# Hybrid streaming encoder on one core: operand buffers at first write, one scratch buffer per builder, and sums given to the engine that ends first

## The chip, the cores and the metric

The kernel runs on one core of a Trainium2 chip. The metric is device time in microseconds of one execution. Three runs of the kernel before gave 2709.64 to 2714.51 us, median 2712.25.

## The reference, cut to what matters

Two layers run over 1024 prompt tokens and 32 sample tokens (1056 columns in all), model width 1024. Each layer has a normalised input projection, latent attention beside retention, an output projection, then the feed-forward part and a gated embedding. The feed-forward part comes once per layer, behind the output projection:

```python
mix = jnp.concatenate([att, retention_out(ret, rg, ret_gn_w[i])], axis=-1)
hp = hp + mix @ w_out[i]                                  # output projection
u = rms_norm(h, norm_ffn_w) @ w_ff1                       # 1024 -> 4096
h = h + jnp.square(jax.nn.relu(u)) @ w_ff2                # 4096 -> 1024
gate = jax.nn.sigmoid(rms_norm(h, norm_ple_w) @ w_ple_gate)
return h + (p_i @ w_ple_proj) * gate
```

## The kernel before, in words

**A planner writes the program.** The Python code of the kernel carries a model of the five engines (`Model`, line 72; `Engine.cost`, line 263). Chains of work are generators; `Pipe` steps each when its next operation could start by the model, and the order in which operations are emitted is the order in which each engine executes them. So a wait in the planner (`pipe.wait`, or a `yield` of a condition) is no wait on the chip: it decides behind what an instruction is written. Matmuls are emitted in line and move the planner's clock; DMAs go to SP's queue. Two-operand sums that VectorE (DVE) or GpSimd (POOL) can do are `Either` (line 202), made by `tt(first, ...)` (line 461): the engine listed first is taken if it can start no more than 0.2 us later than the other.

**Numbers.** Every matmul operand is kept as a high and a low half in f16, and a product is three matmuls per 128 rows: high by high, high by low, low by high. A "split" is the pair of instructions that makes the halves: ScalarE (ACT) casts the high half, and a subtraction by DVE or POOL gives the low half.

**The feed-forward products.** Both matrices are multiplied in blocks of two by two with seven products in place of eight. For this the right operands are seven combinations of the four quarters of the activation (y11, y21, y12, y22 and the sums s1 = y21 + y22, s2 = s1 - y11, s3 = y11 - y21, s4 = y12 - s2), called operands 0 to 6 in the order y11, y12, y22, s1, s2, s3, s4, and the weights have seven combinations too. `load_group` (line 801) fetches four weight blocks, makes four sums with `tt(pool, ...)`, and writes seven weight tiles by `put`. Products are done in the order 1, 7, 6, 4, 5, 2, 3, reading operands 0, 5, 4, 2, 3, 1, 6. 

**The order of a layer's feed-forward part.** Lines 1783 to 1809: the output projection runs over three token groups (2 x 176 columns each), and behind each group `norm_chain` (line 631) squares the rows (ACT), adds them over partitions (TensorE with ones), takes the power -0.5 (POOL), scales a diagonal (ACT) and spreads it by a product with ones, and then four `four` chains (line 717) write operands "x2": two scaled rows, four sums, and four splits, of which (0,5), (1,2) and (4,6) go as pairs. Then come four blocks e; each has four first groups (`ff1_units`, line 943, writing output operands "r") and four second ones (`ff2_units`, line 965, adding into h). The first two groups of block 0 run together, token group by token group, so two units alternate; all other groups run over two halves of 264 columns. `ff1_chains` (line 870) evacuates the products of a unit, squares them and makes sums and splits: ACT copies the first product to `lo` of scratch Ra, and `c11` (line 915) makes s3 and s2 after s1, splitting them as the pair (4,5).

**Buffers.** The arena has 29 slots of 128 x 2 x 1056 f16, weights have 14 slots, temps (128 x 528 f32) 12. x2 takes 14 arena slots, the output operands of two groups 7, a group's staged weights 1, and during the output projection weights may spill into arena halves ("we"). Line 1880 waits for seven free slots before the output operands of two groups are taken, line 746 for temps and a slot before a `four` starts, and only then line 1884 lets the third group's weights load.

## Time and profile before

| what | value |
|---|---|
| runs, median (lowest to highest) | 2712.25 us (2709.64 to 2714.51) |
| the profiled execution, own time | 2710.96 us |
| its span, first to last instruction | 2709.2 us |
| mean granted TensorE clock | 0.974 |
| instructions | 58534 |

In the views, PE is the matmul side of TensorE, DVE VectorE, ACT ScalarE, POOL GpSimd, SP the DMA queue. Times are microseconds from the span's start. Almost every vector instruction is recorded at line 285 and every matmul at line 476, so rows are told apart by tile names (out<-in), with numbers left out of the names: "x" holds x2, "r" is both a scratch buffer of the norm and an output operand, "ra" and "rb" are scratch of a unit, "st", "o", "mm" and "mx" are PSUM banks.

### The profile page before, as it was taken

How to read it: one execution, taken by the hardware profiler on the slowest of the kernel's cores; microseconds unless marked ns; L12 is line 12 of the kernel's file. 1: busy time of each engine (PE TensorE's matmuls, PEld its weight loads, DVE VectorE, ACT ScalarE, POOL GpSimd, SP SyncE). 2: the span in 40 equal slices, each digit the busy share in tenths (PEclk: the TensorE clock that was granted, in tenths of full speed). 3: DMA queues.
4: the chain of work that ended last, by engine and by line, in shares of the span. 5: the costliest groups of instructions: out<-in, count | busy, mean ns of one | idle time of the engine just before them, and what ended most of it. 6: DMA issues, size and time to landing. Idle time of an engine off the chain costs nothing.

```text
span 2709.2 us, 58534 instructions
## 1 busy us (share of the span) xinstructions
PE 2566.6 (95%) x23322; PEld 2006.0 (74%) x23322; DVE 1866.6 (69%) x4555; ACT 1310.0 (48%) x3277; POOL 1056.2 (39%) x1267
## 2 busy tenths in 40 slices
PE   7998989988999999999999989999799999999997
PEld 4765667768888888887656556777688888888965
DVE  6767776656667585875657677775585766768755
ACT  6533366646345262635445344665462534536342
POOL 7123355654333332433331334564732333333331
PEclk8999989989999999999999999999899999999999
DMA  4201010000111212121112011100011111122112
GB/s 136 71 28 49 17 53 27 21 9 33 51 60 52 67 40 75 43 68 50 56 53 70 9 41 34 58 6 29 13 40 50 57 52 59 53 66 68 56 44 64
DMA packets 87057, 130.53 MB, mean 48 GB/s; under 512 B 11584, under 2 KB 36448, under 8 KB 86784
## 3 DMA queue, kind: packets, MB, share of 16 engines
q1 hardware_dynamic: 86496, 126.25, 15.1%
q8 instruction: 182, 2.98, 0.4%
q14 instruction: 91, 0.75, 0.1%
q10 hardware_dynamic: 288, 0.55, 0.1%
HBM read 116.98 MB, written 7.02 MB: 46 GB/s over the span
## 4 chain that ended last, share of the span: by engine, by line
PE 86%; DVE 8%; POOL 3%; ACT 2%; issue 1%; DMA 0%; DVEq 0%; POOLq 0%; ACTq 0%
PE mm L476 33%; PE o L476 20%; PE st L476 19%; PE mx L476 12%; DVE r L285 3%; POOL x L285 1%; PE st L483 1%; PE mx L483 1%; DVE ra L285 1%; DVE w L285 1%; POOL r L285 1%; DVE sf L285 0%; DVE mt L285 0%; PE mm L483 0%; DVE h L285 0%
## 5 line engine op out<-in xcount | busy, mean ns | idle before, releaser
L476 PEld LDWEIGHTS <-w 128*128 128x128 f16 x13176 | 1276.5, 99 | 315.6 <-issue 50.3
L476 PE MATMUL mm<-w,x 128*128 128x256 f16 (+3 forms) x1920 | 334.9, 326 | 11.6 <-DVE sil L285 6.0
L476 PEld LDWEIGHTS <-x 128*128 128x128 f16 x2304 | 222.0, 99 | 147.7 <-DVE sil L285 10.8
L476 PE MATMUL st<-x,w 128*128 128x264 f16 (+2 forms) x1896 | 247.0, 284 | 19.1 <-ACT ra L285 19.1
L285 DVE SCALAR_TENSOR_TENSOR w<-s,w 128x512 f16<-128x512 f32 (+2 forms) x280 | 216.5, 779 | 16.5 <-ACT w L285 14.9
L476 PE MATMUL mm<-x,w 128*128 128x264 f16 (+2 forms) x1800 | 224.7, 281 | 1.3 <-DVE rb L285 1.3
L285 ACT ACTIVATE w<-t 128x512 f16<-128x512 f32 x186 | 111.0, 623 | 226.3 <-POOL t L285 224.9
L476 PE MATMUL o<-x,w 128*128 128x264 f16 (+1 forms) x1608 | 209.7, 282 | 0.0
L476 PE MATMUL mm<-r,w 128*128 128x264 f16 (+1 forms) x1584 | 189.0, 275 | 20.6 <-DVE r L285 20.6
L285 POOL TENSOR_TENSOR pp<-e,pp 128x512 f16<-128x512 f32 (+1 forms) x160 | 169.9, 1073 | 73.9 <-ACT pp L285 59.4
L476 PE MATMUL o<-r,w 128*128 128x264 f16 (+1 forms) x1584 | 196.4, 275 | 0.0
L285 POOL TENSOR_TENSOR t<-stage,s 128x512 f32<-128x512 f32 x64 | 83.8, 1310 | 279.7 <-DMA stage<-in_wts_dram 242.8
L476 PE MATMUL st<-r,w 128*128 128x264 f16 (+1 forms) x1512 | 187.7, 276 | 0.5 <-DVE r L285 0.5
L285 ACT ACTIVATE w<-s 128x512 f16<-128x512 f32 (+2 forms) x280 | 166.8, 599 | 38.3 <-DMA s<-in_wts_dram 23.6
L285 POOL TENSOR_TENSOR t<-s,t 128x512 f32<-128x512 f32 x64 | 81.6, 1275 | 264.5 <-DVE w L285 234.8
L285 ACT ACTIVATE w<-stage 128x512 f16<-128x512 f32 (+1 forms) x130 | 79.3, 613 | 175.7 <-POOL stage L285 159.0
L285 DVE SCALAR_TENSOR_TENSOR w<-t,w 128x512 f16<-128x512 f32 x186 | 135.0, 734 | 26.6 <-ACT w L285 25.4
L285 DVE SCALAR_TENSOR_TENSOR h<-mm,h 128x264 f32<-128x264 f32 (+4 forms) x184 | 82.7, 449 | 88.2 <-PE mm L476 87.4
L285 POOL TENSOR_TENSOR r<-r 128x176 f32<-128x176 f32 (+2 forms) x94 | 67.6, 729 | 154.9 <-ACT qh L285 73.0
L285 DVE SCALAR_TENSOR_TENSOR h<-o,h 128x264 f32<-128x264 f32 (+2 forms) x150 | 64.1, 429 | 91.6 <-PE o L476 90.6
L476 PE MATMUL mx<-x,w 128*128 128x264 f16 (+2 forms) x984 | 124.4, 282 | 0.8 <-DVE w L285 0.8
L476 PE MATMUL st<-qh,k 97*128 97x256 f16 (+5 forms) x672 | 123.7, 259 | 0.0
(293 smaller groups left out, 5049.6 us busy)
## 6 DMA issues: line engine op xcount, KB each, us to landing
s<-in_wts_dram SPq DMA_DIRECT2D x256, 256.0 KB
stage<-in_wts_dram SPq DMA_DIRECT2D x64, 512.0 KB
out_dram<-r SPq DMA_DIRECT2D x24, 176.0 KB
s<-in_wts_dram SPq DMA_DIRECT2D x20, 192.0 KB
h<-in_xT_dram SPq DMA_DIRECT2D x6, 512.0 KB
s<-in_wts_dram SPq DMA_DIRECT2D x16, 144.0 KB
k<-kr SPq DMA_DIRECT2D x16, 136.1 KB
out_dram<-cn SPq DMA_DIRECT2D x16, 128.0 KB
```

What stands on the lines that cost most here:

```text
L285: x = f(*args, **kw)
L476: keep(nc.tensor.matmul(out, lhsT, rhs, start=start, stop=stop, skip_group_check=skip))
L483: keep(nc.tensor.transpose(out, in_, ident))
```

## The change

- `Either.emit` compares when the two engines would end, not when they could start.
- Output operands get their arena slots in `ff1_units`, at the product whose chain first writes them (operands 2,3 at product 5; 0,1 and 4,5 at product 2; 6 at product 3); the wait for seven free slots is gone. x2's slots are taken all at once as before.
- `norm_chain` takes its two accumulators from the temps in every use, keeps acc[0] as the diagonal, and `four` works in one arena slot without a temp: s2 overwrites y21, s4 overwrites s1 after operand 3 is split. So (4) and (6) are split singly, and the wait for one or six free temps is gone.
- `c11` makes s3 in `lo` as soon as y11 and y21 are there and splits it at once; s2 goes to `up` after s1 and is split singly.
- The third group's weights load when operand 0 of x2 is complete, and the next group is staged in a step of its own, when an arena slot and both staging buffers are free.
- A free half of a spilled weight slot is used before a free weight slot.

```diff
+    def end(self):
+        ins, outs, n = self.engine.parts(self.args, self.kw)
+        return self.when() + self.engine.cost(self.name, ins, outs, n)
...
-        (a if a.when() <= b.when() + self.bias else b).emit()
+        (a if a.end() <= b.end() + self.bias else b).emit()
...
-        if weights.free:
+        if weights.free and not half:
...
-        if hold is None:
-            yield lambda: room(3)
-            acc = [T("acc0"), T("acc1")]
-        else:
-            acc = [hold[:, 0], hold[:, 1]]
+        yield lambda: room(3)
+        acc = [T("acc0"), T("acc1")]
+        if hold:
             ps = yield from take("mx")
...
-        diag = (yield from gT("diag")) if hold is None else acc[0]
+        if hold:
+            drop(acc[1])
+        diag = acc[0]
...
-        def four(k, R, R3):
+        def four(k, R):
...
-            s2, s4 = R3[:, :w], R3[:, w:2 * w]
+            s2, s4 = y21, s1
...
             yield tt(pool, s2, s1, y11, op=ALU.subtract)
             pipe.spawn(split((3,), s1, a, w, dve))
+            pipe.spawn(split((4,), s2, a, w, dve))
+            pipe.spawn(split((1, 2), halves(R2[:, :n]), a, w, pool))
+            yield lambda: 3 in parts
             yield tt(pool, s4, y12, s2, op=ALU.subtract)
-            pipe.spawn(split((4, 6), halves(R3[:, :n]), a, w, dve))
-            pipe.spawn(split((1, 2), halves(R2[:, :n]), a, w, pool))
-            yield lambda: parts[0] == 0
-            drop(R, R3)
+            pipe.spawn(split((6,), s4, a, w, dve))
+            yield lambda: len(parts) == 7
+            drop(R)
...
-                yield lambda: room(1 if g == 0 else 6) and arena.free
-                pipe.spawn(four(k, slot("r", (P, 2, HALF), F32), T("r")))
+                yield lambda: arena.free
+                pipe.spawn(four(k, slot("r", (P, 2, HALF), F32)))
...
+    def room_for(op, *pairs):
+        for pr in pairs:
+            if pr[0] in op["o"]:
+                continue
+            if len(pr) == 2 or not op["shared"]:
+                pipe.wait(lambda: arena.free)
+                op["t"].append(slot(f"op{pr[0]}"))
+                sl = op["t"][-1].rearrange("p a (o t) -> p a o t", o=2)
...
+            def s3():
+                yield from split_ops(op, (5,), lo, a, w, dve)
+                u.got.add("x5")
+
             def c11():
                 pipe.spawn(y11())
+                yield u.has("y21")
+                yield dve.q.tensor_tensor(lo, u.f, up, op=ALU.subtract)
+                pipe.spawn(s3())
                 yield u.has("s1")
-                yield dve.q.tensor_tensor(up, u.f, up, op=ALU.subtract)
-                yield dve.q.tensor_tensor(lo, s1, u.f, op=ALU.subtract)
+                yield dve.q.tensor_tensor(up, s1, u.f, op=ALU.subtract)
                 u.got.add("s2")
-                yield from split_ops(op, (4, 5), halves(Ra[:, :2 * w]), a, w, dve)
-                yield u.has("s4")
+                yield from split_ops(op, (4,), up, a, w, dve)
+                yield u.has("s4", "x5")
                 drop(Ra)
...
                 u.prod(i, name, kind, start)
+                room_for(u.op, *{5: ((2, 3),), 2: ((0, 1), (4, 5)), 3: ((6,),)}.get(i, ()))
                 ff1_chains(u, i, R[:, n * u.w:(n + 1) * u.w])
...
-        def load(n):
+        def load(n, cond=None):
             def after():
+                def wait():
+                    yield lambda: arena.free and len(stages.free) == 2
+                    staged[n + 1] = stage(L, us[n + 1])
                 if n + 1 < len(us):
-                    staged[n + 1] = stage(L, us[n + 1])
+                    pipe.spawn(wait())
             if n < len(us):
                 def wait():
-                    yield lambda: n in staged
+                    yield lambda: n in staged and (cond is None or cond())
...
                 if z % 2 == 0:
-                    pipe.wait(lambda: len(arena.free) >= 7)
-                    rr += operands("r", 2, PAIRS_R)
+                    rr += operands(2)
                 if n < 2:
                     if n == 0:
-                        load(2)
+                        load(2, lambda x2=x2: all(len(x["n"][0]) == 6 for x in x2))
```

## Rows read from the trace of the kernel before

**Rows 1.** The page: busy time of the span, and TensorE's share in 40 slices.
```profile
PE 2566.6 (95%) x23322; PEld 2006.0 (74%) x23322; DVE 1866.6 (69%) x4555; ACT 1310.0 (48%) x3277; POOL 1056.2 (39%) x1267
...
PE   7998989988999999999999989999799999999997
```
**Rows 2.** What TensorE waited for: us in total, times, longest us; longest first.
```profile
PE mm L476 <- DVE r L285: 23.9, 16, 3.5
PE st L476 <- ACT ra L285: 19.1, 2, 9.7
PE o L476 <- ACT acc L285: 14.8, 2, 7.7
...
PE mx L476 <- ACT acc L285: 2.7, 2, 1.5
```
**Rows 3.** Busy time of each engine in windows, then granted clock and DMA.
```profile
600.00:625.00 25.00, 13.83 (x121) 13.68 (x122) 10.66 (x28) 9.98 (x28) 22.54 (x27) 0.64 0.06 22
...
825.00:850.00 25.00, 25.00 (x225) 21.73 (x224) 22.80 (x48) 16.62 (x43) 8.63 (x8) 1.00 0.24 75
...
1925.00:1950.00 25.00, 10.40 (x76) 10.26 (x77) 12.47 (x28) 11.03 (x30) 22.60 (x28) 0.64 0.02 5
```
**Rows 4.** Timeline of TensorE at the first entry: start, us, what, [idle before <-releaser].
```profile
591.38 0.61 PE L476 MATMUL o<-ma,w 128*128 128x352 f16 x3
...
601.71 1.59 PE L476 MATMUL o<-acc,ones 128*128 128x128 f32 x6 [7.74 <-ACT acc L285]
603.09 1.97 PE L476 MATMUL st<-x,w 128*128 128x176 f16 x12
...
608.07 1.07 PE L476 MATMUL mm<-x,we 128*128 128x176 f16 x12
618.61 1.92 PE L476 MATMUL st<-x,w 128*128 128x176 f16 x12 [9.47 <-ACT ra L285]
...
621.76 1.07 PE L476 MATMUL mm<-x,w 128*128 128x176 f16 x12
622.67 1.07 PE L476 MATMUL mm<-x,we 128*128 128x176 f16 x12
```
**Rows 5.** Timeline of GpSimd at the first entry.
```profile
600.37 0.84 POOL L285 TENSOR_TENSOR rs<-rs,pw 128x3 f32<-128x3 f32 x1
...
608.19 5.10 POOL L285 TENSOR_TENSOR r<-r 128x176 f32<-128x176 f32 x5 [2.38 <-DVE r L285]
...
617.79 4.90 POOL L285 TENSOR_TENSOR x<-r,x 128x352 f16<-128x352 f32 x6
```
**Rows 6.** Timeline of ScalarE: the first evacuation, and the third group's weights.
```profile
618.26 0.30 ACT L285 ACTIVATE ra<-st 128x176 f32<-128x176 f32 x1
...
619.05 0.65 ACT L285 ACTIVATE w<-s 128x512 f16<-128x512 f32 x1
...
640.11 0.63 ACT L285 ACTIVATE w<-stage 128x512 f16<-128x512 f32 x1
```
**Rows 7.** Timeline of VectorE at the first entry.
```profile
603.34 4.02 DVE L285 SCALAR_TENSOR_TENSOR r<-h,vec,o 128x352 f32<-128x352 f32 x8 [3.63 <-PE o L476]
607.27 0.52 DVE L285 TENSOR_TENSOR x<-r,x 128x352 f16<-128x352 f32 x1
607.71 2.10 DVE L285 TENSOR_TENSOR r<-r 128x176 f32<-128x176 f32 x8
```
**Rows 8.** Timelines at the second step from first to second products, by engine.
```profile
853.15 1.29 PE L476 MATMUL mm<-r,w 128*128 128x264 f16 x10
856.77 3.14 PE L476 MATMUL mm<-r,w 128*128 128x264 f16 x14 [2.34 <-DVE r L285]
...
848.41 0.94 DVE L285 SCALAR_TENSOR_TENSOR mx<-ra 128x264 f32<-128x264 f32 x1
...
855.04 1.68 DVE L285 TENSOR_TENSOR r<-ra,r 128x528 f16<-128x528 f32 x1
...
853.46 0.64 ACT L285 ACTIVATE r<-ra 128x528 f16<-128x528 f32 x1
```

More of the change, by code (lines that the diff above doesn't have):

```diff
@@ L629, with norm_chain @@
     turn = [0, 0]
-    def norm_chain(g, wbase, done, xs=None, ops=None, final=None, fin=None, hold=None):
+    def norm_chain(g, wbase, done, xs=None, ops=None, final=None, fin=None, hold=False):
         a, w = PG[g]
@@ L654, in squares @@
                 yield lambda: fin is None or k in fin
-                if hold is not None:
+                if hold:
                     yield act.q.activation(halves(ac[:, :n]), hv(k), AF.Square)
@@ L674, in norm_chain @@
         pool.memset(rs, 1.0)
-        if hold is None:
+        if not hold:
             yield Need(model, acc[0][:, :n], acc[1][:, :n])
@@ L687, in norm_chain @@
         yield pool.q.tensor_tensor(rs[:, 4:4 + nt], rs[:, :nt], pw[:, :nt], op=ALU.pow)
-        diag = (yield from gT("diag")) if hold is None else acc[0]
+        if hold:
+            drop(acc[1])
+        diag = acc[0]
         for j, (o, tn) in enumerate(tl):
@@ L694, in norm_chain @@
             mm(pb[:, o:o + tn], ones[:tn, :], diag[:tn, o:o + tn], start=True, stop=True)
-        drop(diag if hold is None else hold)
+        drop(diag)
         rbv = halves(pb[:, :n])
@@ L722, in four, with split @@
             y11, y21, s3, y12, y22, s1 = (r[:, i * w:i * w + w] for r in (R1, R2) for i in range(3))
-            s2, s4 = R3[:, :w], R3[:, w:2 * w]
+            s2, s4 = y21, s1
             yield tt(dve, s1, y21, y22, op=ALU.add)
             yield tt(dve, s3, y11, y21, op=ALU.subtract)
-            parts = [4]
-            def split(*args):
-                yield from split_ops(ops[k], *args)
-                parts[0] -= 1
+            parts = set()
+            def split(which, *args):
+                yield from split_ops(ops[k], which, *args)
+                parts.update(which)
             pipe.spawn(split((0, 5), R1.rearrange("p (o t) -> p o t", o=3)[:, ::2], a, w, pool))
@@ L765, with operands @@
     PAIRS_X = ((0, 5), (1, 2), (4, 6), (3,))
-    PAIRS_R = ((0, 1), (2, 3), (4, 5), (6,))
-    def operands(name, nk, pairs):
-        out, single = [], None
-        for k in range(nk):
-            op = {"t": [], "p": {}, "o": {}, "n": [set() for _ in range(7)]}
-            for pr in pairs:
-                if len(pr) == 2 or k % 2 == 0:
-                    op["t"].append(slot(f"{name}{k}{pr[0]}"))
-                    sl = op["t"][-1].rearrange("p a (o t) -> p a o t", o=2)
-                if len(pr) == 2:
-                    op["p"][pr] = sl
-                    op["o"][pr[0]], op["o"][pr[1]] = sl[:, :, 0], sl[:, :, 1]
-                else:
-                    single = sl if k % 2 == 0 else single
-                    op["o"][pr[0]] = single[:, :, k % 2]
-            out.append(op)
-        return out
+    def operands(nk):
+        out = [{"t": [], "p": {}, "o": {}, "n": [set() for _ in range(7)], "z": k % 2} for k in range(nk)]
+        for k in range(0, nk, 2):
+            out[k]["shared"] = out[k + 1]["shared"] = []
+        return out
+    def room_for(op, *pairs):
[6 more added lines that the diff above has]
+                sl = op["t"][-1].rearrange("p a (o t) -> p a o t", o=2)
+            if len(pr) == 2:
+                op["p"][pr] = sl
+                op["o"][pr[0]], op["o"][pr[1]] = sl[:, :, 0], sl[:, :, 1]
+            else:
+                if not op["shared"]:
+                    op["shared"].append(sl)
+                op["o"][pr[0]] = op["shared"][0][:, :, op["z"]]
     def stage(layer, u):
@@ L1783 @@
         pipe.wait(lambda: len(arena.free) >= 18)
-        x2 = operands("x2", KT // 2, PAIRS_X)
+        x2 = operands(KT // 2)
+        for op in x2:
+            room_for(op, *PAIRS_X)
         x2done = set()
@@ L1791 @@
             fin = set()
-            pipe.spawn(norm_chain(g, vb + V_FFN, x2done, ops=x2, fin=fin, hold=slot("acc", (P, 2, HALF), F32)))
+            pipe.spawn(norm_chain(g, vb + V_FFN, x2done, ops=x2, fin=fin, hold=True))
             for m in range(KT):
```

3 lines of the change are left out of this document (1 added, 2 removed).

## The prediction, blind

> **What bounds the kernel now.** I read the page first: TensorE is busy 95% of the span, and of its forty slices few fall below 9 [rows 1]. So a change pays only where TensorE stands still or runs at its lower clock. The list of what TensorE waited for [rows 2] shows two kinds of place with real money. Three of its lines belong to one spot that occurs once per layer, the entry of the feed-forward part: 2.7 us on the last squares, 14.8 us on the scaled diagonal ("o" on ACT acc, twice) and 19.1 us on the first evacuation ("st" on ACT ra, twice), 36.6 us together. The fourth, "mm" on DVE r, 23.9 us in 16 waits, is the step from a block's first products to its second ones: eight such steps hold nearly all of it. The windows put both in place [rows 3]: at the entries TensorE is busy 13.83 and 10.40 us of 25 with a granted clock of 0.64 on average, while in the steady stretch between it is busy 25.00 of 25, with VectorE at 22.80.
>
> The TensorE timeline of the first entry [rows 4] gives the shape. The output projection ends at 592.0 (T0 below). The diagonal product comes at 601.71, the first four feed-forward products run to 609.1, and the next starts at 618.61. At full clock products come 0.91 us apart (621.76 to 622.67), at 1.2 GHz about twice that; the fourth starts 4.98 us after the first, and at 618.61 two more take 3.15: the lower clock costs (4.98 - 2.73) + (3.15 - 1.82) = 3.6 us more. Per entry that is 18.3 idle + 3.6 = 22 us, **44 us in both layers**.
>
> Why it waits: ScalarE makes the copy that frees the bank, ra<-st, only at 618.26 [rows 6], though its product began at 603.09. ScalarE executes in the written order, and the copy was written behind the norm chain's splits. It stands there because line 1880 waits for seven free arena slots. Of 29, x2 holds 14, spilled weights 4 (eight halves) and the third group's stage 1: ten are left for output operands and scratch. Four scratch buffers of the last token group make that six, so the planner waits until one of them is dropped. GpSimd is the slow part of this: its power op comes at 600.37, over eight us after T0, and its sums queue up to 622.7 [rows 5].
>
> **The entry, part by part.** With buffers at first write nothing gates the first products; they can be written directly behind the output projection. Token groups 0 and 1 give 2 x 14 products of 0.91 us, so TensorE has 25.5 us of work from T0 while the last token group is normalised. Is that long enough? I count vector work by what an instruction holds its engine: 0.26 us on VectorE for 176 columns (eight in 2.10), 0.44 for 352 (607.27 to 607.71), 0.50 for the scaled rows (eight in 4.02) [rows 7]; on GpSimd 0.82 for 352 columns (six in 4.90) [rows 5], and, by that price per column with a fixed part, I estimate 0.55 for 176.
> - Work only VectorE can do until then: 12 instructions per unit in four units, 48 x 0.26 = 12.5, plus eight scaled rows 4.0 and one left over 0.5: 17.0 us.
> - Work either can do, in VectorE time: the last group's 16 sums and 12 single splits 28 x 0.26, its 8 paired splits 8 x 0.44, together 10.8 (the 4,6 pair now goes as two singles: 4 ScalarE and 4 vector instructions more per token group, counted here); what is left of group 1 about 7.9 (an estimate: GpSimd's stretch up to the power op and behind it, halved, plus VectorE's part); the units' own four splits, 16 x 0.26 = 4.2. Sum 22.9; on GpSimd it takes twice as long.
>
> If both engines ran freely, T - 17.0 + T/2 = 22.9 gives T = 26.6 us: 1.1 us of idle. If two-operand instructions of the two excluded each other, VectorE has T - 17 for them and GpSimd only the other 17.0, worth 8.5: T = 31.4, 5.9 us of idle. The rows lie near the second: GpSimd's five sums at 608.19 took 5.10 us where 2.75 would do, while VectorE ran its eight sums at full rate [rows 5, 7]. I take 5 us. The Trainium skill (SBUF — State Buffer, section "Who interferes with whom") has that as a rule: an instruction with two SBUF inputs and a GpSimd instruction exclude each other, and the loser blocks fully; by it the idle would be 5.9 us.
>
> With 2 us for the slower clock behind such a gap, 7 us per entry stay: **gain 44 - 14 = 30 us**. Ends: no gap left, gain 44; gap unchanged, gain 0.
>
> The sums going to the engine that is done first matter just here: with both free, GpSimd took a sum it listed first; now VectorE takes it if it ends more than 0.2 us sooner. What is late next is the seventh output slot (rival 1) and the third weight group. That one's load no longer follows line 1884 at once but the last group's split of operand 0, about T0 + 25 = 617, against 619.05 now; its last weight came 21 us later [rows 6], which would be 638, while its seven products start at about T0 + 40 = 632 and come 2.7 us apart, the last at 648. Its transfers are long in; only the next group's, on SP's queue, move with the end of this load, and SP has nothing urgent behind them. Cost 0, covered by 10 us.
>
> **From first to second products.** At 853.15 TensorE stops two products short of the end of operand 5 of the last unit, and resumes at 856.77, when VectorE has written the pair (4,5) low half [rows 8]. The pair had to wait for s2, hence for s1. Now s3 needs only y11 and y21, and y11 is there at 849.3 [rows 8]: its own chain is subtract, ScalarE cast, low half, three short steps, finished some 3 us sooner. Operand 4 is next; it is read two products of 264 columns, 2.7 us, later, and its split is half as long (264 instead of 528 columns). But its sum has the same start as before. I let 1.25 us stay per step: 23.9 - 8 x 1.25 = 14: **gain 14 us**, ends 0 (operand 4 inherits the wait) and 20.
>
> **Costs.** Splitting (4,5) adds one ScalarE and one vector instruction per unit, 68 of each in all; ScalarE took 0.64 for 528 columns [rows 8], so two singles cost about 0.15 more, 10 us in sum. TensorE's full windows [rows 3] hide it; uncovered it would be those 10 us. VectorE there has 2.2 of 25 us spare and will now also draw builders' sums; I charge **4 us**, between 0 and 10 (rival 3 goes beyond).
>
> Diagonal in acc[0] instead of a new buffer, accumulators in temps instead of the arena, half slots before free weight slots, no wait for six temps: 0, each only changes which buffer is taken while ten temps are free; the last chain of the program might move by 2 us either way. The norms at the start of both layers use the same choice of engine: 0, between -4 and +4, as the list, longest first, has their tiles behind its three large lines [rows 2].
>
> **Sum**: against the profiled execution's 2710.96 us, -30 - 14 + 4 gives 2671; the median of the runs is 1.3 us higher, so **2672 us**.
>
> **Rivals.**
> 1. The seventh slot. Seven outputs and four scratch buffers do not fit into ten slots. The shared buffer of operand 6 is asked for last, at T0 + 12; if the last group has taken its four scratch buffers by then (its diagonal may come at T0 + 5), the planner stands until one is dropped, and writes the next copies behind it, as now. From diagonal to copy took 15 us [rows 4, 6], so until T0 + 20 or a little more; TensorE runs ahead to T0 + 16. Some 4 to 5 us of idle, and as much again from the delayed vector work behind it: 9 us per layer, 2690 us. For it speaks the count; against it that group 1's buffers may come back in time.
> 2. Giving sums to the other engine does not shorten the queue. If a sum held the shared port as long on either engine, 22.9 us would count 45.8, T would be beyond 45, and the entry gap would stay as it is: only the second term remains, 2710.96 - 14 + 4, 2702 us by the median. Against it are the 0.26 and 0.55 us of the same sum [rows 5, 7]. The Trainium skill (Perfetto Trace Analysis, section "Optimizing Scalar/DVE Operations") warns that offloading between these two might not help, because they share a read port; by it this rival would be the likely one, and the trace speaks against it.
> 3. Slower. In the steady stretch VectorE has 2.2 of 25 us free [rows 3], 1.66 us in the 18.9 us of one group (14 products of 0.91 x 264/176 = 1.35). Four builder sums of a group on VectorE would be about 2.8 us (an estimate from 0.44 us for 352 columns), the extra splits 0.4: 1.5 us too much in 28 groups, 43 us; with copies for TensorE's banks queued behind them I price it at 2.3 us per group, 64 us: 2735 us. It decides from 1.6 us per group on. Against it: the planner compares ends and gives a sum to VectorE only when its own queue is short.
> 4. The planner's order at the entry hardly moves, because another wait (five free temps, the third group's weights) ends as late: 2711 us. Little speaks for it, with ten temps free.
>
> **How the numbers follow.** The forecast has 0.58, rival 1 0.20, rival 2 0.07, rival 3 0.10, rival 4 0.05. The range goes from 2645 (entry gap closed, 20 us from the steps) to 2704, which takes in rivals 1 and 2; outside are rivals 3 and 4. A measurement can tell about 0.2%, 5.4 us. Faster by more: forecast, rival 1 and rival 2, 0.85; within: rival 4, 0.05; slower: rival 3, 0.10.
>
> **What would show it.** Right: the first feed-forward product starts within 1 us of the output projection's end, the "o" on ACT acc and "st" on ACT ra lines go below 5 us, GpSimd is busy less and VectorE more in the entry window, and "mm" on DVE r falls to about 10 us, with a split of operand 5 before s2. Wrong: a wait of over 5 us on ACT or DVE r in the first twenty us after T0 (rival 1), VectorE full in steady windows with TensorE below 25.00 (rival 3), or GpSimd's share at the entry unchanged (rival 2).

## The result, and the profile after

The kernel after took 2738.88 us by the median (2736.32 to 2743.93, four runs) beside 2711.86 us for the kernel before on the same chip: a ratio of 1.0102, 95% interval 1.0083 to 1.0120. It is slower by 27 us. The forecast was 2672 us, faster, with a range that ended at 2704: wrong by sign.

The profiled execution took 2736.32 us with a span of 2734.2, 25.0 more than before. TensorE's idle time, added up over its timeline, went from 132.5 to 155.2 us, so nearly all of the loss shows as time in which TensorE stood still. The page's line of busy times, to be read beside [rows 1]:

```profile
PE 2569.5 (94%) x23322; PEld 2009.4 (73%) x23322; DVE 2012.1 (74%) x5058; ACT 1321.0 (48%) x3363; POOL 623.0 (23%) x864
```

GpSimd lost 433 us of work and VectorE gained 146. What TensorE waited for (us in total, times, longest us), beside [rows 2]:

```profile
PE mm L480 <- DVE op L289: 55.3, 10, 11.5
...
PE o L480 <- DVE r L289: 14.2, 2, 7.1
```

In this kernel the output operands and x2 are both called "op". The three lines of the entry on ACT are gone, as forecast. In their place two waits of 7.1 us ("o" on DVE r) and two of 11.5 us (inside the first line) stand; the other eight waits of the first line are the steps from first to second products. Before, these stops were 1.6 to 3.5 us (20.6 in all); now they are 3.9 to 4.3 us (32.3 in all). Of the 25 us, 14.8 lie in the blocks between the steps of both layers, 9 between the last step of layer 1 and the end of the next output projection, 4.7 behind the last step and 3.7 ahead of the first entry, while the two stretches from an output projection to the next first step became 7.4 us shorter together. Windows of the entry and of the steady stretch (busy time of PE, PEld, DVE, ACT, POOL, granted clock, DMA), beside [rows 3]:

```profile
600.00:625.00 25.00, 14.79 (x168) 14.37 (x166) 23.20 (x68) 16.61 (x57) 6.36 (x9) 0.82 0.01 2
...
825.00:850.00 25.00, 25.00 (x225) 21.75 (x223) 24.20 (x56) 16.74 (x45) 3.75 (x4) 1.00 0.10 33
```

The steady stretch still has TensorE full, though VectorE there is at 24.20 of 25. At the entry the two vector engines have changed places: before, GpSimd was busy 22.54 of 25 and VectorE 10.66.

**The entry.** TensorE's timeline at the first one, beside [rows 4]:

```profile
596.03 1.07 PE L480 MATMUL st<-op,w 128*128 128x176 f16 x12
...
603.19 0.84 PE L480 MATMUL o<-acc,ones 128*128 128x128 f32 x6
...
610.01 1.07 PE L480 MATMUL st<-op,w 128*128 128x176 f16 x12
618.21 1.94 PE L480 MATMUL o<-op,we 128*128 128x176 f16 x12 [7.12 <-DVE r L289]
619.95 1.97 PE L480 MATMUL mm<-op,w 128*128 128x176 f16 x12
633.39 1.92 PE L480 MATMUL mm<-op,we 128*128 128x176 f16 x12 [11.48 <-DVE op L289]
```

The first feed-forward product does follow the output projection at once, at 596.03, and the diagonal product ("o" from acc and ones) fits between others at 603.19. But all products of the first token group, and one more, are done at 611, and then TensorE stands still for 7.12 and, two products later, for 11.48 us. That is 18.6 us, as much as before. VectorE's timeline shows what it did meanwhile:

```profile
607.50 0.57 DVE L289 SCALAR_TENSOR_TENSOR r<-h,vec,o 128x352 f32<-128x352 f32 x1
...
617.09 1.06 DVE L289 SCALAR_TENSOR_TENSOR r<-h,vec,o 128x352 f32<-128x352 f32 x2
...
626.40 0.70 DVE L289 TENSOR_TENSOR t<-stage,s 128x512 f32<-128x512 f32 x1
627.13 0.69 DVE L289 TENSOR_TENSOR stage<-stage 128x512 f32<-128x512 f32 x1
627.74 0.69 DVE L289 TENSOR_TENSOR t<-stage,t 128x512 f32<-128x512 f32 x1
...
633.00 0.34 DVE L289 TENSOR_TENSOR op<-mm,op 128x176 f16<-128x176 f32 x1
```

Bank "o" is free when the eighth scaled row has read it, at 618.15; the eight rows, which took 4.02 us in one go before [rows 7], are now spread over 10.6 us with sums and low halves between them. Bank "mm" waits for one instruction, op<-mm at 633.00: the low half of operand 2, which reads PSUM. ScalarE had its cast done at 609.5, and GpSimd, which could have taken the builders' sums in front, stood idle for 10.16 us and then again while they ran on VectorE:

```profile
609.15 0.31 ACT L289 ACTIVATE op<-mm 128x176 f16<-128x176 f32 x1
```

```profile
624.01 1.64 POOL L289 TENSOR_TENSOR r<-r 128x176 f32<-128x176 f32 x1 [10.16 <-DVE op L289]
633.32 0.52 POOL L289 TENSOR_TENSOR op<-r,op 128x176 f16<-128x176 f32 x1 [7.66 <-ACT op L289]
```

**A step.** TensorE and VectorE at layer 1's third step from first to second products:

```profile
1015.65 3.24 PE L480 MATMUL mm<-op,w 128*128 128x264 f16 x14 [4.03 <-DVE op L289]
...
1011.96 0.68 DVE L289 SCALAR_TENSOR_TENSOR w<-s,w 128x512 f16<-128x512 f32 x1
1012.56 0.68 DVE L289 SCALAR_TENSOR_TENSOR w<-stage,w 128x512 f16<-128x512 f32 x1
1013.16 0.68 DVE L289 SCALAR_TENSOR_TENSOR w<-t,w 128x512 f16<-128x512 f32 x1
1013.76 1.83 DVE L289 TENSOR_TENSOR op<-ra,op 128x264 f16<-128x264 f32 x2
```

TensorE waits for the second of the two low halves of 264 columns (op<-ra, done at 1015.59), and these stand behind three weights' low halves. In the kernel before, the pair's low half ran first, the weights after it:

```profile
1010.54 1.68 DVE L285 TENSOR_TENSOR r<-ra,r 128x528 f16<-128x528 f32 x1
...
1014.40 0.68 DVE L285 SCALAR_TENSOR_TENSOR w<-s,w 128x512 f16<-128x512 f32 x1
```

### The profile page after: what moved, and what is told of

The parts are those of the page before. It is cut to its first block, busy times and chain, and to the rows that moved or that the text cites. A ratio compares the mean times of both kernels' runs of the same rounds, so it can differ in the third digit from the quotient of the medians.

```text
span 2734.2 us, 58504 instructions
## 1 busy us (share of the span) xinstructions
PE 2569.5 (94%) x23322; PEld 2009.4 (73%) x23322; DVE 2012.1 (74%) x5058; ACT 1321.0 (48%) x3363; POOL 623.0 (23%) x864
## 4 chain that ended last, share of the span: by engine, by line
PE 83%; DVE 13%; ACT 2%; issue 1%; DMA 0%; POOL 0%; SPq 0%; DVEq 0%; POOLq 0%; ACTq 0%
PE mm L480 33%; PE o L480 19%; PE st L480 18%; PE mx L480 11%; DVE w L289 2%; DVE op L289 2%; DVE r L289 1%; DVE ra L289 1%; DVE mt L289 1%; PE mx L487 1%; PE st L487 1%; DVE sf L289 0%; DVE t L289 0%; DVE h L289 0%; DVE y L289 0%
## 5 line engine op out<-in xcount | busy, mean ns | idle before, releaser
L480 PE MATMUL mm<-op,w 128*128 128x264 f16 (+1 forms) x3072 | 370.5, 278 | 32.3 <-DVE op L289 32.3
L480 PE MATMUL st<-op,w 128*128 128x264 f16 (+1 forms) x3144 | 384.9, 274 | 0.0
L480 PE MATMUL o<-op,w 128*128 128x264 f16 (+1 forms) x2856 | 357.3, 276 | 0.0
L480 PE MATMUL mx<-op,w 128*128 128x264 f16 (+1 forms) x1608 | 186.6, 272 | 3.2 <-DVE rs L289 3.2
L289 ACT ACTIVATE w<-s 128x512 f16<-128x512 f32 (+2 forms) x280 | 167.2, 601 | 28.9 <-DMA s<-in_wts_dram 19.3
L289 POOL TENSOR_TENSOR t<-stage,t 128x512 f32<-128x512 f32 x24 | 30.6, 1273 | 397.4 <-DVE t L289 397.3
L289 POOL TENSOR_TENSOR t<-stage,s 128x512 f32<-128x512 f32 x30 | 40.0, 1334 | 335.7 <-DVE w L289 305.2
L289 DVE SCALAR_TENSOR_TENSOR h<-st,h 128x264 f32<-128x264 f32 (+2 forms) x150 | 64.0, 429 | 70.7 <-PE st L480 69.9
L289 ACT ACTIVATE e<-st 128x512 f32<-128x512 f32 (+1 forms) x192 | 89.7, 489 | 50.4 <-PE st L480 43.0
L289 POOL TENSOR_TENSOR op<-r,op 128x264 f16<-128x264 f32 (+2 forms) x46 | 34.4, 751 | 340.6 <-ACT op L289 340.6
L289 DVE SCALAR_TENSOR_TENSOR h<-o,h 128x264 f32<-128x264 f32 (+2 forms) x140 | 60.5, 434 | 64.2 <-PE o L480 62.2
L289 DVE TENSOR_REDUCE mt<-mx 128x1 f32<-128x512 f32 (+4 forms) x192 | 100.5, 534 | 7.1 <-PE mx L480 5.6
```

Of the source, the lines that this page charges most:

```text
L289: x = f(*args, **kw)
L480: keep(nc.tensor.matmul(out, lhsT, rhs, start=start, stop=stop, skip_group_check=skip))
```

## The experiments

The change was cut into three parts: the choice of engine by the end (E), the single splits of operands 4 and 5 (C), and the rest, the new buffers with the norm chain and the third group's load (B). Each time stands beside the kernel before of its own round; the median of that varied from 2708 to 2715 us between rounds, so runs of different rounds are compared by their ratios.

**One part undone or done alone.** The kernel after with the old choice (B and C):

```diff
-        (a if a.end() <= b.end() + self.bias else b).emit()
+        (a if a.when() <= b.when() + self.bias else b).emit()
```

> The changed kernel with the one line of the choice put back (the engine that can start first). Theory A, the choice by the earlier end is the whole loss: time below the kernel before, 2685 to 2705 us; VectorE's share in steady windows falls back to that of before, GpSimd is busy over 1000 us again, and the eight steps from first to second products wait under 3.5 us each. Theory B, the single splits of operands 4 and 5 overload VectorE: it stays above 2725 us. Theory C, the first products written ahead of the norm do the harm at the entry: it stays above 2725 us, with over 15 us of idle per entry.

Measured: 2711.81 us, 1.0000 (0.9990 to 1.0009) of before. The kernel before with the end choice alone (E):

> The kernel before with the choice by the earlier end alone. Theory A: slower, 2730 to 2755 us, GpSimd busy falls to about 620 us, the eight steps wait about 4 us each. Theories B and C: within 6 us of the kernel before.

Measured: 2716.04 us, 1.0016 (1.0006 to 1.0027). The kernel after with the pair (4,5) as before (B and E):

```diff
...
-                yield dve.q.tensor_tensor(lo, u.f, up, op=ALU.subtract)
-                pipe.spawn(s3())
                 yield u.has("s1")
-                yield dve.q.tensor_tensor(up, s1, u.f, op=ALU.subtract)
+                yield dve.q.tensor_tensor(up, u.f, up, op=ALU.subtract)
+                yield dve.q.tensor_tensor(lo, s1, u.f, op=ALU.subtract)
                 u.got.add("s2")
-                yield from split_ops(op, (4,), up, a, w, dve)
+                yield from split_ops(op, (4, 5), halves(Ra[:, :2 * w]), a, w, dve)
...
```

> The changed kernel with the unit's third chain as before (s3 and s2 after s1, split as the pair 4,5). Theory A: within 10 us of the changed kernel, 2729 to 2749 us. Theory B: back to 2715 us or less. Theory C: unchanged, about 2739 us.

Measured: 2721.76 us, 1.0030 (1.0019 to 1.0041). The kernel before with the single splits alone (C):

> The kernel before with only the unit's third chain of the change (s3 early, operands 4 and 5 split singly). Theory A, by which this part helps: 2697 to 2710 us, the eight steps wait 1 to 2 us less each. Theory B: 2722 us or more. Theory C: 2712 us.

Measured: 2732.69 us, 1.0080 (1.0064 to 1.0097): the part of the change that was to bring 14 us costs 21 when it stands alone. Without its partners the end choice costs 4. No one of the three theories fits: A fails at all four runs, C at all but the end choice alone, B at the first and the third, and where B has the number, as in the last run, it doesn't have the reason, as shown below. The parts don't add: B and C together cost nothing. Later the buffers alone (B) and the two others (E and C) completed this:

> The kernel after with the old choice of engine and the old paired splits of operands 4 and 5: what is left is the buffers at first write, the builders' one scratch buffer and the wait of load(2). If the parts added up, this would be e1 less what the single splits cost by themselves (21 us): 2690 us, with steps near 2 us each. If the single splits are only dear in the queue of the kernel before (the parts don't add), the steps stay near 2 us, the entry shows the two gaps of e1 (7.4 and 5.9 us), and the time is 2705 to 2715 us.

> The kernel before with the end choice and the single splits, no new buffers. If both costs add (4.4 and 21.1 us): 2737 us, steps of 4 us and more. If the end choice heals the order of the single splits' low halves (the builders' sums leave GpSimd, so that the weights' low halves no longer run slow): steps near 2 us, 2716 to 2722 us. What lies between this and the kernel after (2738.9 us) is what the new buffers give or take under the end choice.

Measured: B alone 2702.30 us, 0.9955 (0.9939 to 0.9972), the only part that gains by itself; E and C 2742.56 us, 1.0100 (1.0085 to 1.0115). B alone shortens each entry: from the end of the output projection to the first product of 264 columns it takes 56.7 and 56.0 us (layer 1 and 2), where before it took 63.7 and 65.1. Its steps are no better than before (from the second on, two stops of 0.4 and 2.8 us each).

**Why the single splits cost.** VectorE is not busier in C alone than before (1867.5 us against 1866.6), so it isn't load. TensorE, VectorE and ScalarE at its third step, and the window around it:

```profile
1013.99 0.39 PE L476 MATMUL o<-r,w 128*128 128x264 f16 x2 [0.31 <-DVE r L285]
...
1021.04 0.60 PE L476 MATMUL mm<-r,w 128*128 128x264 f16 x2 [4.19 <-DVE r L285]
1021.43 2.85 PE L476 MATMUL st<-r,w 128*128 128x264 f16 x12
...
1016.12 1.03 DVE L285 SCALAR_TENSOR_TENSOR w<-s,w 128x512 f16<-128x512 f32 x1
1017.07 1.17 DVE L285 SCALAR_TENSOR_TENSOR w<-stage,w 128x512 f16<-128x512 f32 x1
1018.16 1.17 DVE L285 SCALAR_TENSOR_TENSOR w<-t,w 128x512 f16<-128x512 f32 x1
1019.25 1.74 DVE L285 TENSOR_TENSOR r<-ra,r 128x264 f16<-128x264 f32 x2
...
1013.44 0.72 ACT L285 ACTIVATE r<-ra 128x264 f16<-128x264 f32 x2
...
1008.00:1034.00 26.00, 21.50 (x165) 17.32 (x163) 18.14 (x38) 9.88 (x24) 10.04 (x9) 0.87 0.19 56
```

The casts are done at 1014.2, the low halves begin at 1019.25, and the three weights' low halves lie between. Behind the stop the clock is lower, too: the twelve matmuls of a product take 2.85 us, and the window's granted clock is 0.87. In the kernel before the same step stopped TensorE for 2.47 us and its window had a clock of 1.00:

```profile
1012.27 1.74 PE L476 MATMUL mm<-r,w 128*128 128x264 f16 x14 [2.47 <-DVE r L285]
...
1002.00:1028.00 26.00, 23.53 (x210) 20.33 (x208) 19.37 (x42) 9.88 (x23) 10.61 (x10) 1.00 0.21 70
```

But the third step is only one of eight. Behind four of the stops of the kernel before the clock fell as well (behind the one of [rows 8] fourteen matmuls took 3.14 us, at the third step 1.74); in C alone it fell behind all eight. The first line of TensorE in C alone shows a second, smaller stop at the step, 0.31 us here and up to 1.0 at others; it ends with another low half (r<-mx). Over the eight steps these smaller stops are 0.5 us in the kernel before and 4.8 in C alone.

So the theory was the order, not the number of instructions. It was tried by holding a weight's low half back while a unit's splits of 4 and 5 are open, in the kernel of C alone:

```diff
+    open45 = [0]
     def put(W, i, src):
...
         yield act.q.activation(w[:, 0], src, AF.Copy, scale=SW)
+        yield lambda: open45[0] == 0
         yield dve.q.scalar_tensor_tensor(w[:, 1], src, SW, w[:, 0], op0=ALU.mult, op1=ALU.subtract)
...
                 yield from split_ops(op, (5,), lo, a, w, dve)
                 u.got.add("x5")
+                open45[0] -= 1
...
+                open45[0] += 2
                 pipe.spawn(s3())
...
                 yield from split_ops(op, (4,), up, a, w, dve)
+                open45[0] -= 1
```

> The kernel before with the single splits of operands 4 and 5 (as e4, 2732.7 us), and a weight's low half isn't put into VectorE's queue while a unit's splits of 4 and 5 are open. Theory of the order (the two low halves stand behind three weight low halves at each step): the idle time at the steps falls from 3.6 to 4.9 us to 1.5 to 2.5 us, the clock behind them stays up, and the time is 2710 to 2718 us. Theory of the count (two casts and two low halves of 264 cost more than one of 528 in any order): the steps stay above 3 us and the time at 2728 to 2736 us. A third way: the weights become late instead, and the idle time goes to <- r,w from weights elsewhere, 2720 us and more.

Measured: 2695.43 us, 0.9929 (0.9914 to 0.9944), better than the theory's own forecast. Nearly the same instructions (VectorE runs 4603 where it was 4599) in another order are 1.5% faster than C alone, some 40 us, and 19 us faster than before. The step, TensorE and then VectorE:

```profile
1006.27 0.39 PE L476 MATMUL o<-r,w 128*128 128x264 f16 x2 [0.31 <-DVE r L285]
...
1010.00 0.39 PE L476 MATMUL mm<-r,w 128*128 128x264 f16 x2 [0.88 <-DVE r L285]
1010.23 1.51 PE L476 MATMUL st<-r,w 128*128 128x264 f16 x12
...
1008.39 1.56 DVE L285 TENSOR_TENSOR r<-ra,r 128x264 f16<-128x264 f32 x2
...
1012.13 0.68 DVE L285 SCALAR_TENSOR_TENSOR w<-s,w 128x512 f16<-128x512 f32 x1
```

The low halves are first, the weights behind them, and the stop is 0.88 us; the smaller one stays. Over the eight steps the two kinds add up to 6.0 and 5.1 us, 11.2 together, where the kernel before has 21.2 and C alone 35.7. The clock falls behind none of them: in windows of 26 us round each stop it is 1.00 throughout, against 0.87 to 0.93 at four steps of the kernel before and at all eight of C alone. Taken as time, these windows lost some 9 us before and 18 in C alone (an estimate, 26 us times what is missing to 1.00); idle and clock together give the two differences to within a few us. From step to step a block takes 152.7 to 153.1 us, where C alone took 157.4 to 158.8. How much of this is the holding back itself? The same line with the pair (4,5), on the kernel before:

> The kernel before (operands 4 and 5 split as a pair), only with the weights held back while that split is open. If e6's gain was all due to holding back, this gives the same as e6, near 2695 us. If the single splits are themselves the gain of e6 (operand 5 ready some us earlier, once nothing stands ahead of it), the steps stay near 2 us and the time is 2706 to 2713 us.

Measured: 2706.07 us, 0.9971 (0.9960 to 0.9982), as its second theory had it. So holding back gives some 8 us to the pairs; with it the single splits are worth about 11 us more, without it they cost 21. The prediction's reason for them holds only when nothing is written ahead of them.

**Why the entry kept its gap.** `Either.when` gives the earlier of the two engines' times. With the end choice a sum is due as soon as GpSimd is free, and is then written into VectorE's queue if it would end sooner there. Work that VectorE alone may do, such as the low half that frees bank "mm", comes behind. The rival was that VectorE had too much to do in any order. The kernel after, with a sum due when the engine that takes it is free:

```diff
     def when(self):
-        return min(op.when() for op in self.ops)
+        return self.pick().when()
     def emit(self):
-        a, b = self.ops
-        (a if a.end() <= b.end() + self.bias else b).emit()
+        self.pick().emit()
+    def pick(self):
+        a, b = self.ops
+        return a if a.end() <= b.end() + self.bias else b
```

> The kernel after with one line changed: a sum that goes to the engine done first is due when that engine is free, not when either is. Theory of starvation (a sum counts as ready as soon as GpSimd is free, is then written into VectorE's queue ahead of the low halves that only VectorE may run, and those hold PSUM banks): the low half of operand 2 at the entry moves from 633 us to before 622 us, the gap of 11.5 us behind the first token group shrinks to under 5 us at both entries, and the time falls to 2718 to 2728 us. Theory of load (VectorE has too much to do there in any order): the gap stays over 8 us, the time within 4 us of 2738 us.

Measured: 2721.76 us, 1.0033 (1.0020 to 1.0046), against 1.0102 for the kernel after: 17 to 19 us less, as the theory of starvation forecast. The first entry, the waits of TensorE and, on VectorE, the last scaled rows and the low half of operand 2:

```profile
617.21 1.08 PE L483 MATMUL st<-op,we 128*128 128x176 f16 x12 [1.55 <-DVE r L292]
623.08 1.92 PE L483 MATMUL mm<-op,w 128*128 128x176 f16 x12 [4.78 <-DVE rb L292]
630.36 1.92 PE L483 MATMUL o<-op,w 128*128 128x176 f16 x12 [3.60 <-ACT ra L292]
...
615.11 2.04 DVE L292 SCALAR_TENSOR_TENSOR r<-h,vec,st 128x352 f32<-128x352 f32 x4
617.08 0.57 DVE L292 TENSOR_TENSOR op<-mm,op 128x176 f16<-128x176 f32 x2
```

The low half moved from 633.00 to 617.08, and the idle time of the entry from 18.6 to 9.9 us per layer: the time lost there was in good part a matter of order as well. The line moved some work, too: over the whole program GpSimd has 748 us in place of 623. But in the 25 us from 604 on, as far behind the output projection as 600 to 625 in the kernel after, VectorE is busy 24.25 us against 23.20 there, so that it isn't the emptier engine that brings the low half forward. The steps stayed at 3.85 us, with a second stop of 0.3.

**Both orders mended.** The kernel after with the weights held back, then with both corrections, and the buffers and single splits with the old choice and the weights held back:

> The kernel after, whole, with the weights' low halves held back while splits of 4 and 5 are open. Theory that the order at the steps is the larger part of its loss: idle time at the steps 4 us to under 2 us, the entry unchanged (7.1 and 11.5 us), 2710 to 2722 us. Rival: under the end choice it is the sums that VectorE has taken over, not the weights' low halves, that stand ahead of the splits; then the steps stay above 3 us and the time above 2730 us.

> The kernel after with both corrections of the order: weights held back (as e6) and a sum due when the engine that takes it is free (as e7, 2721.8 us, entry gaps 9.9 us, steps 3.85 us). If the two are separate losses they add: steps under 2 us, entry gaps near 10 us, 2698 to 2706 us, faster than before. If what is left at the steps of e7 is VectorE's load: steps above 3 us, 2716 to 2724 us.

> The new buffers and the single splits with the old choice of engine (e1, 2711.8 us, steps of 3.2 and 1.5 us) and the weights held back. By the theory of the order the steps fall to 1 to 1.5 us and 2686 to 2697 us come out, the fastest so far; if e1's steps come from something else (GpSimd's share), 2706 to 2714 us.

Measured: 2699.94 us, 0.9951 (0.9935 to 0.9968), steps of 1.0 to 1.3 us and the entry unchanged at 18.0; 2687.33 us, 0.9906 (0.9891 to 0.9920), steps with stops of 0.3 and 0.87 and entry waits of 9.9; 2693.66 us, 0.9929 (0.9913 to 0.9944). The first two are faster than either of their theories had it; the third has the time of its first theory, but its steps still stop TensorE for 2.4 us, not 1 to 1.5. What TensorE waits for at the steps of the kernel with both corrections:

```profile
PE st L483 <- DVE op L292: 7.0, 8, 0.9
...
PE mm L483 <- DVE op L292: 2.3, 8, 0.3
```

One line that holds back the weights thus takes some 40 us off the kernel after, a second correction another 13, and the whole change so mended is 0.9% faster than before. VectorE is still busy 1993.6 us in it, 127 more than before.

What do the new buffers contribute to that? The same without them, that is the kernel before with E, C and both corrections:

> e10 (2687.3 us) without the new buffers: the kernel before with the end choice, a sum due when its own engine is free, the single splits and the weights held back. Theory that the first products run ahead of the norm only with the buffers at first write, and that this is worth its time once the order is right: the entry shows about 15 us idle per layer in place of 9.9, and the time is 2695 to 2703 us. If the buffers are worth nothing (as e11 against e6, 1.8 us apart, suggests): 2684 to 2691 us.

Measured: 2688.40 us, 0.9913 (0.9898 to 0.9927), not to be told from the 2687.33 us with them. Its first entry on TensorE:

```profile
598.07 0.78 PE L483 MATMUL mx<-ones,acc 128*128 128x1 f32 x6 [1.20 <-ACT acc L292]
598.71 1.07 PE L483 MATMUL o<-x,w 128*128 128x176 f16 x12
```

The first product is at 598.71 right behind the projection, although the wait for seven free slots stands as in the kernel before, and the products of 264 columns begin 55.4 and 55.3 us after the projection, as with the new buffers (55.3 and 55.2). With the end choice alone, too, the first product follows the projection at once (599.19).

Next, the corrected kernel with the builders' four sums given back to GpSimd:

```diff
-            yield tt(pool, t1, b12, b11, op=ALU.subtract)
+            yield pool.q.tensor_tensor(t1, b12, b11, op=ALU.subtract)
```

(and the other three sums alike)

> e10 with the builders' four sums fixed to GpSimd, as nearly all were before; the end choice stays for the norm's and the units' sums. If VectorE's load is what is left at the entry and at the steps: VectorE's busy time falls by some 100 us, the entry gaps (9.9 us) shrink by the 2 to 3 us of sums in front of them, and the time is 2676 to 2684 us. If GpSimd's sums and VectorE's two-operand work hold each other up as much as they are worth: 2685 to 2692 us. Slower than 2692 us would say that the builder's sums on GpSimd come late for the weights.

Measured: 2684.86 us, 0.9903 (0.9886 to 0.9920), between its two theories and not to be told from 2687.33. Waits of TensorE at the first entry, and the window:

```profile
613.91 1.08 PE L483 MATMUL o<-op,we 128*128 128x176 f16 x12 [3.30 <-DVE r L292]
618.12 1.07 PE L483 MATMUL st<-op,w 128*128 128x176 f16 x12 [1.31 <-ACT ra L292]
633.44 1.92 PE L483 MATMUL mm<-op,we 128*128 128x176 f16 x12 [3.33 <-DVE rb L292]
...
600.00:625.00 25.00, 20.38 (x264) 20.03 (x263) 23.52 (x71) 16.99 (x60) 13.89 (x20) 1.00 0.01 2
```

The clock stays at 1.00 and the entry takes 49.1 us in both layers. But the steps are worse again: the first of each layer has no stop left, the other six have three each (1.83, 0.66 and 0.77 us at the second step), 17.2 us in all where the kernel with both corrections has 9.3.

**The choice outside the feed-forward part.** From the last step of layer 1 to the end of the next output projection, the kernel before took 755.0 us and the kernel after 764.1. All runs with the end choice had over 760 there, those without it 752 to 755. Behind the last step of layer 2 it is alike: 214.7 to 217.6 us with the end choice as in the kernel after, 209.6 to 213.4 in all others. So the end choice was kept for the feed-forward part alone, in the kernel with both corrections, and in the same with the builders' sums on GpSimd:

```diff
+    ff = False
     def when(self):
-        return self.pick().when()
+        return self.pick().when() if Either.ff else min(op.when() for op in self.ops)
...
         a, b = self.ops
+        if not Either.ff:
+            return a if a.when() <= b.when() + self.bias else b
...
+        Either.ff = True
         x2 = operands(KT // 2)
...
+        Either.ff = False
         final = L == DEPTH - 1
```

> e10 (2687.3 us) with the end choice and its due time only from the first layer's x2 on to the last second product of each layer; elsewhere (attention, norms of the gate part, both layers' starts) the old choice. In every run with the end choice everywhere, the stretch from the fourth step of layer 1 to the end of the output projection of layer 2 took 761 to 769 us, in every run without it 752 to 755. If the end choice is what costs there: that stretch returns to 752 to 756 us, the first output projection ends near 592 us, and the time is 2672 to 2679 us. If that stretch follows from the feed-forward part before it (the state in which it leaves the queues), it stays over 760 us and the time at 2685 to 2690 us.

> e14 (2684.9 us, builders' sums on GpSimd) with the end choice in the feed-forward part alone. The same two theories: 2669 to 2677 us, or 2682 to 2688 us. Its entries should stay at 49 us each and its steps at 2.7 to 3.3 us in both.

Measured: 2680.00 us, 0.9893 (0.9870 to 0.9917), and 2676.38 us, 0.9881 (0.9854 to 0.9909). The stretch took 754.7 and 756.2 us, as without the end choice: it is the choice that costs there. The times alone would not show it, as both intervals overlap with those of the kernels without this restriction (0.9891 to 0.9920 and 0.9886 to 0.9920). The first output projection ended at 596.4 and 593.0 us; it differs by 4.5 us between kernels that choose alike up to there (592.0 to 596.5 among those with the old choice), so the 3.7 us of the kernel after can't be put down to anything. The second of the two has the lowest ratio of this study, 1.2% below the kernel before. What TensorE waits for in it, longest first:

```profile
PE mm L487 <- DVE sil L296: 13.5, 12, 3.8
PE o L487 <- DVE op L296: 8.8, 6, 1.8
PE o L487 <- DVE r L296: 6.6, 2, 3.3
PE mm L487 <- DVE rb L296: 6.4, 2, 3.3
```

The first line is in the attention part, which no experiment touched; the entry (third and fourth line) is down to 13 us in both layers.

The entries side by side, from the end of the output projection to the first product of 264 columns, read from TensorE's timeline, with the idle time in it:

| kernel | layer 1, us (idle) | layer 2, us (idle) |
|---|---|---|
| before | 63.7 (19.3) | 65.1 (19.0) |
| after | 62.0 (18.6) | 62.2 (18.6) |
| buffers alone | 56.7 (13.4) | 56.0 (13.5) |
| after, sums due with their engine | 54.4 (9.9) | 54.4 (9.9) |
| both corrections | 55.3 (10.6) | 55.2 (10.5) |
| both, without the buffers | 55.4 (12.9) | 55.3 (12.9) |
| both, builders' sums on GpSimd | 49.1 (7.9) | 49.1 (7.9) |
| the same, end choice in the feed-forward part alone | 49.3 (6.6) | 47.7 (6.4) |

## Why the prediction was wrong

**What bounds the kernel: right for the gains, not for the loss.** The entries and the steps are where the corrections gained. But of the 25 us lost, 14.8 lie in the blocks with the steps and 13.8 behind each layer's last step (9.1 and 4.7), which the prediction held to be nearly untouched; the stretch with the entry became shorter.

**From first to second products: the step that failed first.** "Its own chain is subtract, ScalarE cast, low half, three short steps, finished some 3 us sooner" gave a gain of 14 us. The chain was right in its parts but was counted as if nothing stood between them. VectorE works in the order written; three weights' low halves were written between the cast and the low half. Each stop grew by about 1.5 us in the kernel after, and the clock fell behind seven of the eight, where before it fell behind four. With the weights held back the mechanism came out, and most of the size: the steps' idle time is 11.2 us (single splits on the kernel before) and 9.3 (both corrections) where there were 21.2, a gain of 10 and 12 us for the 14 forecast. The 14 started from 23.9 us, of which 3.3 are waits outside the eight steps. The clock at the steps, which the prediction's sum left out, brought about as much again: some 9 us, by the estimate above. The prediction also took 853.15 for the start of the stop [rows 8]; ten matmuls run from there on, and what is left behind the stop is two matmuls of that product, not two products. Which instructions stand ahead is shown by both timelines and by the experiment; why the planner writes them there for single splits and not for a pair wasn't tried.

**The entry: the gate opened, the sum failed.** "Nothing gates the first products" held. "If the two-operand instructions of the two excluded each other ... 5.9 us of idle" treated VectorE's work as a sum in which the order doesn't matter, and counted no builders' sums and no weights in it. In the kernel after 18.6 us of idle stayed, of which 11.5 hung on one instruction of 0.34 us that was written behind other work, sums that GpSimd could have run among it. With both orders mended and the builders' sums on GpSimd the two entries are 14.6 and 16.0 us shorter than before, together the 30 us of the forecast; but that kernel's steps are worse, so the two forecast gains appear each in another kernel, and none has both in full.

**The cause of the gate: half right.** "It stands there because line 1880 waits for seven free arena slots" named the wait, and the prediction called GpSimd the slow part of it, but the gain was put down to the buffers. With the end choice alone, and with all but the buffers, the first product follows the projection at once although the wait for seven slots stands; that the slots then come free in time is read from the code, not from a trace. Buffers alone remove the gate as well, but the two gains are one and the same.

**Costs and rival 3.** The rival that ended slower had 2735 us, close to what was measured, for another reason: VectorE overloaded in the steady stretch. TensorE stayed full there, and the corrected kernel has nearly the same load on VectorE (1993.6 against 2012.1 us) and is 52 us faster. The 0.10 for it was too little, as "slower" had a second way that the prediction lacked: an order in which the instruction that TensorE needs stands behind others. Rival 4 (the order hardly moves) did not come about. The sign set for rival 1 did, a wait of over 5 us on DVE r in the first twenty us (7.12 us, from 611.1 on, 15.4 behind the projection), but it ended with the eighth scaled row, which frees bank "o"; with the same buffers and the sums due with their engine it is 1.55 us, so the seventh slot was not what held it. (The lower end of the range, 2645, is 3 us below what its own terms give, 2648; nothing hangs on it.)

**Rival 2 and the warning on offloading.** The Trainium skill (Perfetto Trace Analysis, section "Optimizing Scalar/DVE Operations") says that moving work between the two engines might not help. For the end choice alone this case agrees: GpSimd went from 1056 to 656 us of work and the kernel took 1.0016 of the time. The reason that the page gives, the shared port, is not shown to be the one here. In that kernel the steps' idle time fell from 21.2 to 13.5 us, while the stretch behind layer 1's last step grew by 8 us and the one behind layer 2's by 4; why it grew there was not tried.

**The choice elsewhere, "0, between -4 and +4": mis-sized.** The stretch of the second layer's start, with the gate part ahead of it, was 9.1 us longer in the kernel after, and the last two runs show that the choice of engine is why; what in it costs the time there stays open. The 4.7 us behind the last step go with the choice, too, but no run was made for them alone. The reason given, that the waits on these tiles stood behind three large lines, spoke of waits there were, not of waits that a new order would make.

## What to carry to other kernels

Splitting an instruction so that its first half is ready sooner gains only if the queue it is written into lets it go first; look up what stands between cast and low half in the timeline of the engine, not only how long each takes. When a planner chooses between engines, the time at which a job counts as due must be that of the engine which will run it, or jobs that had a choice are put ahead of jobs that have none. And when a wait is for buffers, ask which engine is late in giving them back before giving it more of them.

## What the runs showed of the hardware

A stop of TensorE can cost more than its length, as the clock may fall behind it, and in these runs the length alone doesn't tell whether it will. Behind the eight stops of the kernel before, 1.6 to 3.5 us long, the granted clock stayed at 1.00 four times and fell to the lower of its two levels four times; a stop of 2.47 us is among the first and one of 2.34 among the second. In the kernel after a stop of 3.90 us left it at 1.00, while in C alone it fell behind all eight of 3.6 to 4.9 us, and with the weights held back behind none of those under 0.9. Where it fell, the next twelve matmuls of 264 columns took up to 2.85 us instead of 1.51. What decides between the two is not shown.

A weight's low half took 0.68 us at the step of the kernel before and 1.17 us in the single-split kernel, where GpSimd ran a sum or a low half at the same time. In the whole kernel before, 418 such low halves had no sum or split of GpSimd beside them and took 0.67 to 0.69 us; the other 134 took up to 1.78. The Trainium skill (SBUF — State Buffer, section "Who interferes with whom") calls the port pair that the two engines share an exclusive lock. The trace agrees as far as it goes: at that step the two took turns, VectorE starting at 1016.12, 1017.07 and 1018.16, GpSimd at 1016.56, 1017.65 and 1018.74. So the order costs twice there: more stands ahead, and it runs slower.
